# A Hymba-style encoder layer in split fp32r: one later norm sum, one more f with merged products, and two down units moved to the end of an f

## The chip, the cores and the metric

One core of one Trainium2 chip. The time is device time in microseconds for one execution, the median of 3 runs. Beside the runs there is one profiled execution, from which every view is taken; its times are given from the start of its span.

## The reference, cut to what matters

The kernel computes one encoder layer on 512 tokens of width 2048 and a last RMSNorm, all in float32. The first half (a norm, one input projection, a convolution group and a neighbourhood attention group, an output projection) is left as it is. What the change touches is the gated MLP behind it:

```
xn = rms_norm(x, ffn_norm_g)                 # 512 x 2048
up = xn @ w_up                               # 512 x 11264, gate half and value half
up = depthwise_conv(up, ffn_dw_w, ffn_dw_b)  # width 3 along the tokens
gate, val = split(up)
x = x + (silu(gate) * val) @ w_down          # 5632 -> 2048
return rms_norm(x, final_norm_g)
```

## The kernel before, in words

**Split operands.** Each float32 factor is split into a high part (rounded to fp32r) and a low part (the rest), and a product is three matmuls: high by high, high by low, low by high. For a weight unit (128 x 1024 numbers, 512 KB) ScalarE makes the high part `whi` (L117) and VectorE the low part `wlo` (L121). There are four buffers of each. `weights()` (L158) hands out units in the order of the list `plan` and makes each three units ahead of its use.

**The up projection.** The 5632 columns of each half are 44 tiles of 128, called f (0 to 43); eleven chunks c of four f (i = 0 to 3) share a down projection. For one f, the gate and the value tile by the two halves of the depth and of the tokens are combined into seven products, 0 to 6, as in Strassen's scheme as Winograd writes it; seven combinations `comb[c]` of the input stand in SBUF, each with high and low part beside each other, 256 columns each. A product has eight steps k over the depth. Three of the seven weight units are sums of loaded ones, made under names `ws` and `raw`: unit 1 and 2 by L712 and L714, unit 4 by L719, unit 6 by L723, on VectorE. Where f is 4 or less, `sums()` (L694 to L698) lets DMAs that add do the first two.

**Two forms of a product.** `up_apart` (L853) uses three matmuls of 256 columns for each k (lines 131, 135 and 136): high by high, high by low, low by high, all into one half of a PSUM bank. `up` (L764) is the merged form: one matmul of 512 columns by the high part (L774, "wides") gives high by high in the left half of the bank and high by low in the right half, and one of 256 columns (L780, "lows") adds low by high to the right half. Each product then comes out as two halves that are still to be added; that takes more copies on ScalarE (L810) and more additions on VectorE (L825 to L849, against L884 to L890). In the merged form the products are in runs that open together: (0,1), (2,3), (4,5), (6) for f under 4, and (0,1,2,3), (4,5,6) from f=4 on. The high matmuls of all products of a run come first (of the last one only the first), then the low ones product by product, each followed by the rest. f=0 and f=3 use `up_apart`, all others `up`.

**Gating.** `gated_tile` (L906) multiplies by the second norm's factor `rstd2` (L907, L908), does the width-3 convolution (L897 on ScalarE, L898 and L899 on VectorE), the SiLU (L910) and the product (L911). `in_two` (L914) splits the result into `hh` (L916, ScalarE) and `hl` (L917, VectorE). In the first chunk all four are split behind f=3.

**The down projection.** A down unit is one weight unit and two of the 16 output tiles d: 16 matmuls with the high weights (L934, hh and hl in turn), 8 with the low ones (L944), then for each d a copy out of PSUM (L946, ScalarE) and a DMA from POOL's queue that adds it to `x2d` in DRAM (L947). The two PSUM banks come from the tag `tr` (L924). `down_units(c, i, at)` (L732) says which units of the chunk before come behind product `at` of the f with index i; the same function places their weights in `plan`. Up to the last chunk one unit stands behind product 3 and one behind product 6 of each f.

**The second norm.** `stats2` (L678) runs beside f=0: behind each product `tick` (L141) lets it go one step. At the third step it adds two loaded sums (L684) and splits the result (L189, L190); after `rest` further steps two matmuls by ones (L194) sum over the partitions, and ScalarE and VectorE make `rstd2` (L198 to L205).

**What sets the order.** Each engine works off its own queue in order. A planner orders the queues beforehand, by the order of the code as priority and by costs and due times that it assumes; only instructions that are pinned, and those that `issue_after` ties to a matmul, are fixed by hand. The PE instructions of the up and down projections are not pinned. Loads of weights are on SP's queue (L112).

Of the kernel before, what the change touches and what calls it, by code (L numbers as in the profile page):

```python
# [17 lines left out]
D = 2048  # L18
# [24 lines left out]
CH = 4  # L43
# [23 lines left out]
def layer(ctx: ExitStack, tc: tile.TileContext, xT, xG, xw, w_a, w_in, w_v, w_out, w_up, w_down, par, tab, g3, out, last_out):  # L67
# [17 lines left out]
    def t2(name, dt=F32):  # L85
        return tp.tile([P, S], dt, tag="t2k", name=name)
# [54 lines left out]
    def tick(behind, mid=False):  # L141

        for todo in (steps, asteps):
            while todo and mid == (todo is asteps and amid[0]):
                try:
                    with tc.issue_after(behind.ins):
                        at = next(todo[0])
                    if todo is asteps:
                        amid[0] = at == "mid"
                    break  # L150
                except StopIteration:
                    todo.pop(0)
# [5 lines left out]
    def weights():  # L158
        at = weights.at
        weights.at += 1  # L160
        while len(made) < min(at + 1 + AHEAD, len(plan)):
            made.append(plan[len(made)]())
        return made[at]
# [21 lines left out]
    def spread(acc, to, n, name, bank, hold=False, both=False):  # L185

        m = to.stop - to.start
        h, l = (t2("n" + c, F32R)[:, :m] for c in "hl")
        nc.scalar.activation(h, acc[:, to], AF.Copy)  # L189
        nc.vector.tensor_sub(l, acc[:, to], h.bitcast(F32))  # L190
        yield
        ps = bank()[:, :m]
        for i, x in enumerate((h, l)):
            x = nc.tensor.matmul(ps, ones_r, x, start=i == 0, stop=i == 1)  # L194
            if i or hold:
                pin(x)
        r, q = t2(name)[:, :m], t2("q")[:, :m]
        nc.scalar.activation(r, ps, AF.Abs_reciprocal_sqrt, scale=1.0 / n, bias=eps)  # L198
        nc.vector.scalar_tensor_tensor(q, r, -0.5 / n, r, op0=ALU.mult, op1=ALU.mult)
        nc.vector.scalar_tensor_tensor(q, ps, n * EPS, q, op0=ALU.add, op1=ALU.mult)  # L200
        if both:
            nc.vector.scalar_tensor_tensor(ps, q, 1.5, r, op0=ALU.add, op1=ALU.mult)
            nc.scalar.activation(r, ps, AF.Copy)
            return ps, r
        nc.vector.scalar_tensor_tensor(r, q, 1.5, r, op0=ALU.add, op1=ALU.mult)  # L205
        return r

    def stat_bank(free=False):
        if free:
            return psa.tile([P, 2, S], F32, tag="sc", name="st")[:, 0]  # L210
        return psa.tile([P, S], F32, tag="po", name="st")

    def factor(acc, n, name, rest=1, free=False):
        steps = spread(acc, slice(0, S), n, name, lambda: stat_bank(free))
        next(steps)
        for _ in range(rest):
            yield
        try:
            next(steps)
        except StopIteration as e:  # L220
            return e.value
# [24 lines left out]
    for k in range(KD):  # L246
        if k < CH:
            raw = t4([P, U * P], "raw")
            n = S + 2 * P + (0 if k else KD)
# [3 lines left out]
        else:  # L253
            if k % CH == 0:
                raw = t4([P, U * P], "raw")
            if k % CH == 0 or k == CH + 2:
                o, n = 2 * (k % CH) * P, 2 * (2 if k < 2 * CH else CH) * P
# [22 lines left out]
    for step in ORDER:  # L280
# [5 lines left out]
        i = next(a_ if step == "a" else q_)  # L286
# [280 lines left out]
    p, n = -1, 0  # L567
# [104 lines left out]
    rstd2 = []  # L672
# [5 lines left out]
    def stats2():  # L678
        acc2, q = t2("acc2"), t2("sq")
        nc.sync.dma_start(acc2, sq2[0])  # L680
        nc.sync.dma_start(q, sq2[1])
        yield
        yield
        nc.vector.tensor_add(acc2, acc2, q)  # L684
        rstd2.append((yield from factor(acc2, D, "rstd2", rest=2, free=True)))

    def factors(f):

# [43 lines left out]
    def down_units(c, i, at):  # L732

        n = U // CH
        if not c:
            return ()
        if c < NCH - 1:
            return {3: (4 * i,), 6: (4 * i + n,)}.get(at, ())
        return {(1, 3): (0,), (1, 6): (2,), (2, 3): (4,), (2, 6): (6,), (3, 6): range(8, KD, n)}.get((i, at), ())
# [10 lines left out]

    out_half(mb, after)
    steps.append(stats2())

    def product_bank(f, c):

        n = 7 * f + c
        at = n % 6 if f < CH else 3 * (c % 3 == 0 and c > 0)
        if at < 3:
            return psm.tile([P, S], F32, tag="mm", name="pu")
        if at == 3:  # L760
            return psa.tile([P, S], F32, tag="po", name="pu")
        return psa.tile([P, S], F32, tag="tr", name="pu", bufs=2)

    def up(f, between):  # L764

        opened = {}
        runs = ((0, 1), (2, 3), (4, 5), (6,)) if f < CH else ((0, 1, 2, 3), (4, 5, 6))

        def bank(c):
            return product_bank(f, c)  # L770

        def wides(c, w, ps, ks, stop=False):
            for k in ks:
                i = nc.tensor.matmul(ps, w[0][:, k * P:(k + 1) * P], comb[c][k], start=k == 0,  # L774
                                     stop=stop and k == ks[-1])
            return i

        def lows(c, w, ps, stop=False):
            for k in range(U):
                i = nc.tensor.matmul(ps[:, H:], w[1][:, k * P:(k + 1) * P], comb[c][k][:, :H], start=False,  # L780
                                     stop=stop and k == U - 1)
            return i

        def product(c):

            w = weights()
            run = next(r for r in runs if c in r)
            if len(run) == 1:
                ps = bank(c)
                wides(c, w, ps, range(U - 1))  # L790
                lows(c, w, ps)
                i = wides(c, w, ps, range(U - 1, U), stop=True)
            elif c == run[-1]:
                ps = opened.pop(c)
                lows(c, w, ps)
                i = wides(c, w, ps, range(1, U), stop=True)
            else:
                if c == run[0]:
                    for j in run:
                        opened[j] = bank(j)  # L800
                        wides(j, w if j == c else made[weights.at + j - c - 1], opened[j],
                              range(1 if j == run[-1] else U))
                ps = opened.pop(c)
                i = lows(c, w, ps, stop=True)
            tick(i)
            between(c)
            return ps[:, :H], ps[:, H:]

        def copy(to, ps):
            nc.scalar.activation(to, ps, AF.Copy)  # L810

        def pair(name):
            return t2(name).rearrange("p (i t) -> p i t", i=2)

        def both(x):
            return x.unsqueeze(1).broadcast_to([P, 2, H])


        vv, low = pair("vv"), pair("pl")
        for i in range(2):  # L820
            m, l = product(i)
            copy(vv[:, i], m)
            copy(low[:, i], l)
        m7, l = product(2)
        add(vv, vv, low)  # L825
        low = pair("pl")
        copy(low[:, 0], l)
        m1, l = product(3)
        copy(low[:, 1], l)
        uu, v = pair("uu"), pair("vl")  # L830
        u, u2 = uu[:, 0], uu[:, 1]
        add(u2, m7, low[:, 0])
        add(v, vv, both(u2))
        m6, l = product(4)
        add(u, m1, low[:, 1])
        low = pair("pl")
        copy(low[:, 0], l)
        add(u2, u, m6)
        m2, l = product(5)
        add(u2, u2, low[:, 0])  # L840
        add(v, v, both(u2))
        add(vv[:, 1], vv[:, 1], u2)
        low, g = pair("pl"), pair("g")
        copy(low[:, 0], l)
        add(g[:, 0], u, m2)
        m3, l = product(6)
        copy(low[:, 1], l)
        add(g[:, 1], vv[:, 1], m3)
        add(g, g, low)  # L849
        g, v = (t.rearrange("p i t -> p (i t)") for t in (g, v))  # L850
        return g, v
# [49 lines left out]
        return y  # L901

    def hidden(f, between):
        return gated_tile(f, *(up_apart if f == CH - 1 else up)(f, between))

    def gated_tile(f, g, v):  # L906
        nc.vector.tensor_mul(g, g, rstd2[0])  # L907
        nc.vector.tensor_mul(v, v, rstd2[0])  # L908
        g, v = conv3(g, f), conv3(v, NF + f)
        nc.scalar.activation(g, g, AF.Silu)  # L910
        nc.vector.tensor_mul(g, g, v)  # L911
        return g
# [38 lines left out]
    def behind(c, i, at):  # L951
        if c == NCH - 1 and (i, at) == (0, 3):
            pend[-1] = in_two(pend[-1])
        down(pend, down_units(c, i, at))
# [23 lines left out]
    n = CH  # L978
# [47 lines left out]
    for d in range(KD):  # L1026
# [3 lines left out]
        i = nc.vector.tensor_add(x2[d][:, fm], x2[d][:, fm], ps)  # L1030
# [24 lines left out]
    for g, ps in enumerate(banks):  # L1055
# [5 lines left out]
        for k in range(n):  # L1061
# [3 lines left out]
            i = nc.tensor.matmul(ps, hh[:, tm], dh, start=False, stop=False)  # L1065
# [104 lines left out]
```

## Time and profile before

| | us |
|---|---|
| median of 3 runs | 2012.88 |
| lowest, highest | 2012.29, 2012.9 |
| the profiled execution's own time | 2013.73 |
| its span, first to last instruction | 2011.8 |
| f=0 begins, f=4 begins (first matmul) | 661.84, 742.97 |

In rows of the timeline the first number is the start, the second how long the group lasts, then engine, line, operation, what it writes and reads, shapes, and how many are grouped; in brackets stands the idle time of the engine ahead of it and what ended that. PE is TensorE's matmuls, PEld its weight loads, DVE is VectorE, ACT ScalarE, POOL GpSimd, SP SyncE. Matmuls overlap, so the printed length of one is longer than the distance to the next. In rows of windows come the stretch, its length, the busy time and instruction count of PE, PEld, DVE, ACT and POOL, the clock granted to TensorE, the share of the DMA engines and GB/s.

### The profile page before, as it was taken

What the parts mean: (1) busy time and instruction counts of PE and PEld (TensorE: products, weight loads), DVE (VectorE), ACT (ScalarE), POOL (GpSimd) and SP (SyncE); (2) the same over time, 40 slices, a digit from 0 to 9 for tenths busy, and PEclk for the clock granted to TensorE, in tenths of its full rate; (3) what the DMA queues carried; (4) which work ended last, traced back from release to release, by engine and by line L of the source; (5) the groups of instructions that cost most, each with busy time, mean ns of one, the idle gap of its engine ahead of it and who ended that gap; (6) DMA issues with size and microseconds to landing.
All of it is one profiled execution on the core that took longest, in us unless ns stands there. A gap on an engine that the chain in (4) does not pass through costs nothing.

```text
span 2011.8 us, 28094 instructions
## 1 busy us (share of the span) xinstructions
PE 2001.2 (99%) x10510; PEld 1716.8 (85%) x10510; DVE 1659.2 (82%) x2264; ACT 1065.7 (53%) x1689; POOL 171.1 (9%) x201
## 2 busy tenths in 40 slices
PE   9999999999999999999999999999999999999998
PEld 8888888888888898888888888888888888888887
DVE  7996888988576898887888888888887888888875
ACT  6323344476356665555655555564655655555563
POOL 0000000000002101111111111111111111110111
PEclk9999999999999999999999999999999999999999
DMA  7232323346348765555556555555555565564574
GB/s 258 84 105 92 112 96 110 105 138 209 104 136 211 187 159 156 135 136 149 132 133 149 134 134 148 135 136 147 133 139 147 131 142 147 131 142 126 147 200 136
DMA packets 98567, 284.25 MB, mean 141 GB/s; under 512 B 11008, under 2 KB 11520, under 8 KB 98432
## 3 DMA queue, kind: packets, MB, share of 16 engines
q1 hardware_dynamic: 71712, 231.07, 36.0%
q0 software_dynamic: 26720, 51.40, 16.8%
q8 instruction: 83, 1.36, 0.3%
q14 instruction: 52, 0.43, 0.1%
HBM read 227.90 MB, written 54.53 MB: 140 GB/s over the span
## 4 chain that ended last, share of the span: by engine, by line
PE 97%; DMA 1%; DVE 0%; ACT 0%; issue 0%; ACTq 0%; POOL 0%; POOLq 0%; DVEq 0%; SPq 0%
PE pu L774 27%; PE pu L780 14%; PE pd L934 14%; PE pd L944 7%; PE pj L131 6%; PE pj L135 6%; PE pj L136 6%; PE po L131 3%; PE po L135 3%; PE po L136 3%; PE pv L341 1%; PE pv L340 1%; PE pv L342 1%; PE pd L136 1%; PE pd L135 1%; PE pd L131 1%
## 5 line engine op out<-in xcount | busy, mean ns | idle before, releaser
L117 ACT ACTIVATE whi<-raw 128x1024 fp32r<-128x1024 f32 x364 | 384.8, 1058 | 537.6 <-PE pd L934 138.5
L121 DVE TENSOR_TENSOR wlo<-raw,whi 128x1024 fp32r<-128x1024 f32 x364 | 444.6, 1222 | 224.6 <-PE pu L780 101.2
L774 PE MATMUL pu<-xc,whi 128*128 128x512 f32 x2352 | 562.8, 390 | 0.0
L774 PEld LDWEIGHTS pu<-xc,whi 128*128 128x128 f32 x2352 | 435.9, 188 | 87.0 <-issue 0.2
L780 PEld LDWEIGHTS pu<-xc,wlo 128*128 128x128 f32 x2352 | 293.9, 192 | 6.8
L780 PE MATMUL pu<-xc,wlo 128*128 128x256 f32 x2352 | 296.1, 283 | 0.0
L934 PE MATMUL pd<-hl,whi 128*128 128x512 f32 x608 | 236.5, 389 | 0.0
L934 PE MATMUL pd<-hh,whi 128*128 128x512 f32 x608 | 236.5, 389 | 0.0
L947 POOL DMA_DIRECT2D x2d<-pdc x160 | 140.6, 895 | 1093.1 <-ACT pdc L946 1086.1
L131 PE MATMUL pj<-xh,whi 128*128 128x512 f32 x512 | 198.4, 392 | 0.1
L136 PE MATMUL pj<-xh,wlo 128*128 128x512 f32 x512 | 198.2, 390 | 0.0
L135 PE MATMUL pj<-xl,whi 128*128 128x512 f32 x512 | 198.2, 390 | 0.0
L117 ACT ACTIVATE whi<-ws 128x1024 fp32r<-128x1024 f32 x132 | 140.0, 1061 | 102.6 <-PE pu L774 54.2
L810 ACT ACTIVATE pl<-pu 128x256 f32<-128x256 f32 x294 | 111.4, 380 | 125.3 <-PE pu L774 88.0
L396 DVE SCALAR_TENSOR_TENSOR y<-ch,prm,y 128x501 f32<-128x501 f32 (+14 forms) x240 | 173.8, 743 | 4.4
L121 DVE TENSOR_TENSOR wlo<-ws,whi 128x1024 fp32r<-128x1024 f32 x132 | 161.3, 1222 | 3.3 <-ACT whi L117 1.9
L944 PE MATMUL pd<-hh,wlo 128*128 128x512 f32 x608 | 150.1, 389 | 0.0
L934 PEld LDWEIGHTS pd<-hl,whi 128*128 128x128 f32 x608 | 114.1, 188 | 23.8 <-DVE hl L917 0.2
L944 PEld LDWEIGHTS pd<-hh,wlo 128*128 128x128 f32 x608 | 114.1, 188 | 23.7
L934 PEld LDWEIGHTS pd<-hh,whi 128*128 128x128 f32 x608 | 114.1, 188 | 23.6
L131 PEld LDWEIGHTS pj<-xh,whi 128*128 128x128 f32 x512 | 96.0, 188 | 20.9 <-ACT whi L236 0.3
L136 PEld LDWEIGHTS pj<-xh,wlo 128*128 128x128 f32 x512 | 96.1, 188 | 20.5
(234 smaller groups left out, 2774.7 us busy)
## 6 DMA issues: line engine op xcount, KB each, us to landing
raw<-in_w_up SPq DMA_DIRECT2D x176, 512.0 KB, 3.6
raw<-in_w_down SPq DMA_DIRECT2D x88, 512.0 KB, 4.0
x2d<-pdc POOLq DMA_DIRECT2D x160, 256.0 KB, 4.9
raw<-in_w_in SPq DMA_DIRECT2D x60, 512.0 KB, 3.6
raw<-in_w_out SPq DMA_DIRECT2D x32, 512.0 KB, 3.6
raw<-in_w_v SPq DMA_DIRECT2D x16, 512.0 KB, 4.1
tab<-in_tab SPq DMA_DIRECT2D x32, 256.0 KB, 4.9
x<-in_xT SPq DMA_DIRECT2D x16, 256.0 KB, 5.6
```

What stands on the lines that cost most here:

```text
L117: i = nc.scalar.activation(hi[:, :n], raw[:, :n], AF.Copy)
L121: j = nc.vector.tensor_sub(lo[:, :n], raw[:, :n], hi[:, :n].bitcast(F32))
L131: m = nc.tensor.matmul(ps, hi[:, a], mh, start=start, stop=False)
L135: nc.tensor.matmul(ps, hi[:, a], ml, start=False, stop=False)
L136: return nc.tensor.matmul(ps, lo[:, a], mh, start=False, stop=stop)
L396: nc.vector.scalar_tensor_tensor(y[:, a:b], h[:, a + j - PAD:b + j - PAD], prm[:, o + j:o + j + 1], y[:, a:b], op0=ALU.mult, op1=ALU.add)
L774: i = nc.tensor.matmul(ps, w[0][:, k * P:(k + 1) * P], comb[c][k], start=k == 0, stop=stop and k == ks[-1])
L780: i = nc.tensor.matmul(ps[:, H:], w[1][:, k * P:(k + 1) * P], comb[c][k][:, :H], start=False, stop=stop and k == U - 1)
L810: nc.scalar.activation(to, ps, AF.Copy)
L934: nc.tensor.matmul(ps, w[0][:, a], x, start=k + i == 0, stop=False)
L944: nc.tensor.matmul(ps, w[1][:, a], hs[k][0], start=False, stop=k == CH - 1)
L947: nc.gpsimd.dma_start(xd[d], t, accum_op=ALU.add)
```

## The change

Three edits. The factor of the second norm waits three steps and not two between the split and the two matmuls that sum it, so these matmuls come one product later in f=0. f=3 uses the merged form `up` like the others, and only f=0 stays in `up_apart`. And in the second chunk's first f (f=4) both down units, 0 and 2, stand behind product 6, where the first of them stood behind product 3; their weights move in `plan` likewise. Behind the edit in `down_units` the lines of the new kernel are two further down.

```
-        rstd2.append((yield from factor(acc2, D, "rstd2", rest=2, free=True)))
+        rstd2.append((yield from factor(acc2, D, "rstd2", rest=3, free=True)))
...
     def down_units(c, i, at):
         n = U // CH
         if not c:
             return ()
+        if c == 1 and not i:
+            return (0, n) if at == 6 else ()
         if c < NCH - 1:
             return {3: (4 * i,), 6: (4 * i + n,)}.get(at, ())
...
     def hidden(f, between):
-        return gated_tile(f, *(up_apart if f == CH - 1 else up)(f, between))
+        return gated_tile(f, *up(f, between))
```

More of the change, by code (lines that the diff above doesn't have):

```diff
@@ L684, in stats2 @@
         nc.vector.tensor_add(acc2, acc2, q)
-        rstd2.append((yield from factor(acc2, D, "rstd2", rest=2, free=True)))
+        rstd2.append((yield from factor(acc2, D, "rstd2", rest=3, free=True)))
     def factors(f):
@@ L736, in down_units @@
             return ()
+        if c == 1 and not i:
+            return (0, n) if at == 6 else ()
         if c < NCH - 1:
@@ L903, in hidden @@
     def hidden(f, between):
-        return gated_tile(f, *(up_apart if f == CH - 1 else up)(f, between))
+        return gated_tile(f, *up(f, between))
     def gated_tile(f, g, v):
```

## The prediction

> **What bounds the kernel now.** I read the page's busy times first, then the chain that ended last.
>
> ```profile
> PE 2001.2 (99%) x10510; PEld 1716.8 (85%) x10510; DVE 1659.2 (82%) x2264; ACT 1065.7 (53%) x1689; POOL 171.1 (9%) x201
> PE 97%; DMA 1%; DVE 0%; ACT 0%; issue 0%; ACTq 0%; POOL 0%; POOLq 0%; DVEq 0%; SPq 0%
> ```
>
> TensorE is busy 99% of 2011.8 us and is 97% of the chain, so a change can win only by giving it less to do or by closing one of its few waits. An 82% VectorE looks idle enough, but that is a mean over stages. The table of windows, cut where the first f's begin, shows the stretch that the diff touches (columns: stretch, length, busy time of PE, PEld, DVE, ACT, POOL):
>
> ```profile
> 703.40:722.90 19.50, 19.50 (x114) 17.22 (x113) 18.89 (x27) 11.47 (x19) 1.73 (x2) 1.00 0.65 170
> 722.90:743.00 20.10, 20.10 (x170) 20.10 (x169) 19.53 (x27) 10.21 (x14) 1.74 (x2) 1.00 0.73 190
> 743.00:773.40 30.40, 30.40 (x163) 26.15 (x162) 30.03 (x40) 18.65 (x29) 1.78 (x2) 1.00 0.52 150
> 773.40:803.70 30.30, 30.30 (x161) 26.22 (x160) 24.64 (x32) 16.73 (x25) 3.50 (x4) 1.00 0.56 140
> ```
>
> These are f=2, f=3, f=4 (with two down units) and f=5. VectorE is full up to 773.4 (30.03 of 30.40 us) and has 5.66 us to spare from f=5 on. So here two engines are bound together, and what matters is by how much VectorE's weight parts come ahead of TensorE's use of them.
>
> **The norm's sum.** The timeline of PE, and of DVE, at the end of the fifth product of f=0:
>
> ```profile
> 676.11 0.28 PE L136 MATMUL pu<-xc,wlo 128*128 128x256 f32 x1
> 676.65 0.49 PE L194 MATMUL st<-nh,ones 128*128 128x512 f32 x1 [0.26 <-ACT nh L189]
> 677.72 0.50 PE L194 MATMUL st<-nl,ones 128*128 128x512 f32 x1 [0.58 <-DVE nl L190]
> 678.06 0.28 PE L131 MATMUL pu<-xc,whi 128*128 128x256 f32 x1
> ...
> 675.24 0.69 DVE L684 TENSOR_TENSOR acc<-acc,sq 128x512 f32<-128x512 f32 x1 [1.96 <-DMA sq<-sq]
> 678.25 1.22 DVE L121 TENSOR_TENSOR wlo<-ws,whi 128x1024 fp32r<-128x1024 f32 x1
> ```
>
> TensorE's price per matmul is the distance of starts, not the printed length:
>
> ```profile
> 687.80 3.82 PE L774 MATMUL pu<-xc,whi 128*128 128x512 f32 x16
> 691.45 2.08 PE L780 MATMUL pu<-xc,wlo 128*128 128x256 f32 x16
> ...
> 722.81 0.28 PE L131 MATMUL pu<-xc,whi 128*128 128x256 f32 x1
> 742.97 5.86 PE L774 MATMUL pu<-xc,whi 128*128 128x512 f32 x25
> ```
>
> Sixteen 512-wide ones take 691.45-687.80 = 3.65 us, 0.228 each. All of f=3, apart, is 7x24 matmuls of 256 columns in 742.97-722.81 = 20.16 us, 0.120 each. From 676.11 to 678.06 are 1.95 us; undisturbed it would be 0.12+2x0.228 = 0.58. The two sum matmuls thus hold TensorE up 1.37 us, because their input comes from a sum that landed by DMA at 675.2. One product later is 676.23+24x0.12 = 679.11, after nl was there (it released the matmul at 677.72): the wait goes whole, **-1.37 us**. What is late next: the seventh product's low part ends at 678.25+1.22 = 679.47, and TensorE would use it at 679.11+0.46+0.24 = 679.81, 0.34 us later. It just fits. rstd2 then comes some 1.4 us later at most; its first readers (L907, L908 for f=0) are far enough behind, and VectorE has other work in between.
>
> **The fourth f merged.** Per k two 256-wide matmuls become one of 512: 2x0.120-0.228 = 0.012 us, 56 times, 0.67 us. I take **-0.67 us**. The page "TensorE: Matmul & The Clock Gate" of the Trainium skill (section "Wait — 56ns, not 53.3ns?") states a time of N/2.4 ns plus about 2.5 ns for each matmul, by which the merge would save only 2.5 ns each, 0.14 us in all (an estimate from that page). The rows give 0.120 us for 256 columns where the page's rule gives 0.109, so the measurement decides.
>
> In exchange there are more additions. Issue distances of VectorE, from the timeline in f=2:
>
> ```profile
> 707.15 0.69 DVE L849 TENSOR_TENSOR g<-g,pl 128x512 f32<-128x512 f32 x1
> 707.75 1.22 DVE L719 TENSOR_TENSOR ws<-ws,raw 128x1024 f32<-128x1024 f32 x1
> ...
> 719.85 1.23 DVE L121 TENSOR_TENSOR wlo<-raw,whi 128x1024 fp32r<-128x1024 f32 x1
> 720.98 0.42 DVE L838 TENSOR_TENSOR uu<-uu,pu 128x256 f32<-128x256 f32 x1
> 721.31 1.23 DVE L121 TENSOR_TENSOR wlo<-ws,whi 128x1024 fp32r<-128x1024 f32 x1
> ```
>
> So 0.60 us for 512 columns, 0.33 for 256, 1.13 for a weight unit. Merged, an f has 4 wide and 7 narrow additions (4.71 us); apart, 2 and 4 (2.52 us): VectorE gets **2.19 us more**, in the stretch where it is full. ScalarE gets six more copies of 0.38 us, 2.3 us, beside 10.21 us of work in 20.10: hidden.
>
> ```profile
> L810 ACT ACTIVATE pl<-pu 128x256 f32<-128x256 f32 x294 | 111.4, 380 | 125.3 <-PE pu L774 88.0 <-PE pu L780 33.1 <-DMA x2d<-pdc 1.1
> ```
>
> **Both down units at the end of f=4.** The work stays the same; the order changes. First the rows of f=4 (PE; then DVE and ACT):
>
> ```profile
> 754.11 0.39 PE L934 MATMUL pd<-hh,whi 128*128 128x512 f32 x1
> ...
> 759.60 4.02 PE L774 MATMUL pu<-xc,whi 128*128 128x512 f32 x17
> 763.45 3.04 PE L780 MATMUL pu<-xc,wlo 128*128 128x256 f32 x24
> ...
> 771.57 1.98 PE L944 MATMUL pd<-hh,wlo 128*128 128x512 f32 x8
> 773.38 1.98 PE L774 MATMUL pu<-xc,whi 128*128 128x512 f32 x8
> ...
> 710.18 1.23 DVE L121 TENSOR_TENSOR wlo<-ws,whi 128x1024 fp32r<-128x1024 f32 x1 [0.61 <-ACT whi L117]
> 737.48 0.42 DVE L886 TENSOR_TENSOR uu<-uu,pu 128x256 f32<-128x256 f32 x1 [0.54 <-PE pu L136]
> 752.01 1.22 DVE L121 TENSOR_TENSOR wlo<-raw,whi 128x1024 fp32r<-128x1024 f32 x1
> 754.89 0.68 DVE L917 TENSOR_TENSOR hl<-uy,hh 128x512 fp32r<-128x512 f32 x1
> 757.23 1.22 DVE L723 TENSOR_TENSOR ws<-ws,raw 128x1024 f32<-128x1024 f32 x1
> 758.48 1.06 ACT L117 ACTIVATE whi<-ws 128x1024 fp32r<-128x1024 f32 x1 [3.78 <-DVE ws L723]
> ...
> 772.78 0.58 ACT L946 ACTIVATE pdc<-pd 128x512 f32<-128x512 f32 x1
> ```
>
> The moved down unit is the 759.60-754.11 = 5.49 us of TensorE between product 3 and product 4. It also was the time in which VectorE caught up. The tightest unit is the seventh (made by L723, then whi, then wlo). Its high part is ready at 758.48+1.06 = 759.54, and TensorE first uses it with the last of the 17 matmuls, at 759.60+16x0.228 = 763.25: 3.7 us to spare.
>
> After the change TensorE wants it 5.49 us earlier for the missing down unit, and 2.04 us earlier for the two gains: 755.72. VectorE reaches L723 at 757.23+2.19-1.13 (the down unit's low part of 752.01, now behind) and, where its two idle moments of 0.61 and 0.54 close, 1.15 sooner: 757.14. The high part then is there at 759.45, **3.7 us late** if every queue keeps the order of the code. Two things can shorten that. The low matmuls of products 4 and 5, 16x0.12 = 1.92 us, need nothing from it and can be queued ahead; the planner, which orders each queue before the run, has done this once, in f=40:
>
> ```profile
> 1844.54 5.40 PE L774 MATMUL pu<-xc,whi 128*128 128x512 f32 x23
> 1849.78 0.63 PE L780 MATMUL pu<-xc,wlo 128*128 128x256 f32 x4
> 1850.38 0.47 PE L774 MATMUL pu<-xc,whi 128*128 128x512 f32 x1
> ```
>
> Here four low matmuls stand ahead of the last of 24 high ones (the rest of product 3 and the 17 that open products 4 to 6), where the code has all the low ones behind it. And the four hl of L917 (4x0.60 = 2.4 us, the last at 754.89) no longer have to be ready at 754: behind L723 they would bring it to 754.7 and leave 1.3 us of lateness. So the cost lies between 0 (both) and 3.7 (neither; 4.9 if the idle moments stay). I take one of them, **+1.9 us**.
>
> A second new wait: the two units now follow each other in the two banks of L924. The second's first matmul needs the first's eviction, which began 1.21 us after the eight low matmuls did (772.78 against 771.57) and ended at 773.36, when they were over at 773.38. So it is 0 with ScalarE free and up to 1.06 with a whi ahead of the copy; I take **+0.1**. The moved unit's SP load (512 KB) and its two POOL transfers of 0.9 us have idle queues around them: POOL is busy 1.78 of 30.40 us.
>
> **Sum:** -1.37-0.67+1.9+0.1 = -0.04 us on the span of 2011.8 (2013.73 for the profiled execution, 0.85 above the median). On the median of 2012.88 that is **2012.8**, no change.
>
> **Rivals.**
> - **The gain survives whole** (low matmuls ahead and hl behind): -2.04+0.1, so 2010.9. For it: no deadline asks for hl before 760 any more. Against it: hl is issued ahead of the later units in the code.
> - **VectorE becomes the bound, slower**: the order of the code, a 3.7 us wait ahead of the high matmul of f=4's seventh unit and 0.3 at the bank: -2.04+4.0 = +2.0, 2014.9 (to 2016.1 with the idle moments unclosed). It decides when L723 starts after 753.4 (755.72 less the 1.25 to whi's start and its 1.06) and nothing is put ahead. For it: DVE's 30.03 of 30.40. Against it: the row of 1849.78.
> - **The wait slows TensorE's clock**: at the start sixteen 256-wide matmuls took 3.50 us, 0.219 each against 0.120, while the granted clock reads 1.00. If a wait of 3.7 us brought that rate back for so many, it adds 16x0.099 = 1.6: 2016.5. The same page of the Trainium skill (section "What's actually happening") says that an idle window of about 3.4 us halves the clock until the engine has again been busy as long. No wait of that length stands in this trace's FFN, so nothing here tests it.
>
> ```profile
> 1.10:4.60 3.50, 3.50 (x16) 3.29 (x16) 0.49 (x2) 1.64 (x4) 0.38 (x2) 1.00 0.81 268
> ```
>
> - **The moved sum gives nothing**: the 0.34 us of room at the seventh product of f=0 goes to a queue shuffle, and -1.37 becomes some -0.3: 2013.9.
>
> **How the numbers follow.** Forecast 0.42, whole gain 0.20, VectorE bound 0.22, slow clock 0.07, sum without gain 0.09. The range is 2010.5 to 2016.0: below lies little of the whole gain (2010.9), above it most of the slow clock and the far end of the second rival, some 0.15 together. A measurement of this kernel tells about 0.2% (4.0 us) from no change. A gain over 4.0 us isn't there to be had, since the waits and matmuls named hold 2.0: 0.02. A loss over 4.0 us takes half of the slow clock's chance (its 3.6 us and a little more) and the far end of the second rival (a wait over 6 us at the seventh unit, with the bank's 1.06 on top): 0.04 and 0.06, so 0.10. The rest, 0.88, is within.
>
> **What would show it.** The profile after should have the st matmuls at 679.1 without a wait, f=3 in 19.45 us, VectorE full until f=5. Then look at f=4's seventh product: a PE wait named for whi L117 is the second rival, low matmuls ahead of it the forecast, no wait the first. A wait on ACT pdc ahead of the second down unit prices the bank. I am wrong if waits appear in f=2 or f=3, where the sixth and seventh units have little room, or if hl, not a weight part, holds the down units.

## The result, and the profile after

The changed kernel takes 2020.55 us (median of 6 runs, 2019.48 to 2021.8), the kernel before 2012.87 beside it (6 runs, 2012.29 to 2013.4): a ratio of 1.0038, 95% interval 1.0028 to 1.0048. That is 7.7 us slower, outside the range of 2010.5 to 2016.0. The profiled execution of after took 2020.29 us with a span of 2018.4; lines of the new kernel from `down_units` on are two further down (L774 is now L776, L810 L812, L835 L837).

The page of after, first the busy times and then TensorE's costliest group (its last columns: busy time, mean ns, idle time ahead of it and what ended most of that):

```profile
PE 2002.2 (99%) x10454; PEld 1714.7 (85%) x10454; DVE 1660.5 (82%) x2269; ACT 1066.2 (53%) x1695; POOL 171.2 (8%) x201
...
L776 PE MATMUL pu<-xc,whi 128*128 128x512 f32 x2408 | 578.1, 391 | 5.6 <-ACT pl L812 2.9
```

TensorE has 56 matmuls fewer, VectorE 5 instructions and ScalarE 6 more, as foretold. New are 5.6 us of idle time ahead of the high matmuls, half of them ended by a copy of ScalarE. The timeline of TensorE, from the norm's sum on, shows where they stand:

```profile
679.16 0.39 PE L194 MATMUL st<-nh,ones 128*128 128x512 f32 x1
679.39 0.39 PE L194 MATMUL st<-nl,ones 128*128 128x512 f32 x1
...
740.75 6.08 PE L776 MATMUL pu<-xc,whi 128*128 128x512 f32 x26
746.67 4.00 PE L782 MATMUL pu<-xc,wlo 128*128 128x256 f32 x32
750.50 1.78 PE L776 MATMUL pu<-xc,whi 128*128 128x512 f32 x7
755.16 5.54 PE L776 MATMUL pu<-xc,whi 128*128 128x512 f32 x16 [2.88 <-ACT pl L812]
763.39 0.47 PE L776 MATMUL pu<-xc,whi 128*128 128x512 f32 x1 [2.70 <-DVE uu L837]
763.70 3.03 PE L782 MATMUL pu<-xc,wlo 128*128 128x256 f32 x24
766.57 1.78 PE L776 MATMUL pu<-xc,whi 128*128 128x512 f32 x7
768.18 0.39 PE L936 MATMUL pd<-hh,whi 128*128 128x512 f32 x1
...
773.66 0.50 PE L936 MATMUL pd<-hh,whi 128*128 128x512 f32 x1
...
779.23 5.83 PE L776 MATMUL pu<-xc,whi 128*128 128x512 f32 x25
```

The first 26 high matmuls are the last of f=3 and 25 of f=4, so f=4 begins 0.23 us into that row, at 740.98, against 742.97 before: 1.99 us were gained. It ends at 779.23 against 773.38: 5.85 us late, so f=4 lost 7.84. From there on the two timelines run 5.85 us apart to the last matmul. The rest of the 6.56 us between the two profiled executions came behind it (9.2 us to the end of the span, against 8.5); the medians differ by more, since the profiled execution of before lay 0.86 above its median.

In f=4 the loss is four terms. The seven matmuls from 750.50 on should be followed at 750.50+7x0.228 = 752.10, and the sixteen of products 4 and 5 start at 755.16: **3.06 us**, released by ScalarE's copy L812. These sixteen take 5.54 us where sixteen took 3.82 in f=1: **1.72**. The first matmul of product 6 follows 2.86 us late, released by VectorE's L837: **2.86**. The rest (0.08 behind that, 0.14 at the second down unit) is **0.22**. Together 7.86, against the 7.84 read from the starts of f=4 and f=5.

Neither release is a weight part. They free banks of PSUM. From f=4 on, products 0, 1, 2, 4, 5 share three banks and products 3 and 6 share one (L759, the tag `po`), so product 4 needs the bank of product 0, emptied by ScalarE's copies L812, and product 6 that of product 3, emptied when VectorE's L837 has read it. ScalarE in after, then in before:

```profile
751.65 0.62 ACT L912 ACTIVATE uy<-uy 128x512 f32<-128x512 f32 x1
752.17 1.14 ACT L918 ACTIVATE hh<-uy 128x512 fp32r<-128x512 f32 x2
753.93 0.63 ACT L918 ACTIVATE hh<-uy 128x512 fp32r<-128x512 f32 x1 [0.62 <-DVE uy L913]
754.46 0.37 ACT L812 ACTIVATE vv<-pu 128x256 f32<-128x256 f32 x1
754.73 0.38 ACT L812 ACTIVATE pl<-pu 128x256 f32<-128x256 f32 x1
```

```profile
752.07 0.37 ACT L810 ACTIVATE vv<-pu 128x256 f32<-128x256 f32 x1
752.33 0.38 ACT L810 ACTIVATE pl<-pu 128x256 f32<-128x256 f32 x1
```

In before the bank of product 0 came free at 752.7 and nobody asked for it till 759.60, behind the down unit. In after TensorE asks at 752.10, and the copies stand behind the rounding L918 of f=3's gated tile, which waits for VectorE's product L913. VectorE's timeline in after, then its one row of before that matters:

```profile
756.14 1.23 DVE L723 TENSOR_TENSOR ws<-ws,raw 128x1024 f32<-128x1024 f32 x1
757.28 0.70 DVE L919 TENSOR_TENSOR hl<-uy,hh 128x512 fp32r<-128x512 f32 x1
757.88 1.23 DVE L712 TENSOR_TENSOR ws<-raw 128x1024 f32<-128x1024 f32 x1
759.01 0.70 DVE L827 TENSOR_TENSOR vv<-vv,pl 128x512 f32<-128x512 f32 x1
759.62 0.43 DVE L834 TENSOR_TENSOR uu<-pu,pl 128x256 f32<-128x256 f32 x1
759.95 1.23 DVE L121 TENSOR_TENSOR wlo<-ws,whi 128x1024 fp32r<-128x1024 f32 x1
761.08 0.69 DVE L835 TENSOR_TENSOR vl<-vv,uu 128x512 f32<-128x512 f32 x1
761.68 1.23 DVE L121 TENSOR_TENSOR wlo<-raw,whi 128x1024 fp32r<-128x1024 f32 x1
762.82 0.43 DVE L837 TENSOR_TENSOR uu<-pu,pl 128x256 f32<-128x256 f32 x1
```

```profile
761.05 0.42 DVE L835 TENSOR_TENSOR uu<-pu,pl 128x256 f32<-128x256 f32 x1
```

VectorE never rests here: each instruction begins as the one before it gives way. L837 is done at 763.25 because eight others stand ahead of it, whatever TensorE does. In before the same addition ended at 761.47, and TensorE wanted the bank at 763.25. In after it wanted it at 760.5, though it had lost nearly 5 us by then.

### The profile page after: what moved, and what is told of

It is laid out like the page before. It is cut to its first block, busy times and chain, and to the rows that moved or that the text cites. A ratio compares the mean times of both kernels' runs of the same rounds, so it can differ in the third digit from the quotient of the medians.

```text
span 2018.4 us, 27994 instructions
## 1 busy us (share of the span) xinstructions
PE 2002.2 (99%) x10454; PEld 1714.7 (85%) x10454; DVE 1660.5 (82%) x2269; ACT 1066.2 (53%) x1695; POOL 171.2 (8%) x201
## 4 chain that ended last, share of the span: by engine, by line
PE 62%; ACT 0%; DVE 0%; ACTq 0%; issue 0%; DVEq 0%
PE pu L776 25%; PE pd L936 14%; PE pu L782 13%; PE pd L946 7%; PE pd L135 1%; PE pd L136 1%; PE pd L131 1%; PE pt L1071 0%; PE pt L1067 0%; PE pt L1070 0%; PE pt L1059 0%; ACT xg L1091 0%; ACT sq L1074 0%; ACTq L1167 0%; PE st L194 0%; DVE uu L837 0%
## 5 line engine op out<-in xcount | busy, mean ns | idle before, releaser
L776 PE MATMUL pu<-xc,whi 128*128 128x512 f32 x2408 | 578.1, 391 | 5.6 <-ACT pl L812 2.9
L776 PEld LDWEIGHTS pu<-xc,whi 128*128 128x128 f32 x2408 | 447.2, 189 | 95.8 <-ACT pl L812 3.3
L782 PEld LDWEIGHTS pu<-xc,wlo 128*128 128x128 f32 x2408 | 301.2, 191 | 7.1
L782 PE MATMUL pu<-xc,wlo 128*128 128x256 f32 x2408 | 303.4, 283 | 0.0
L812 ACT ACTIVATE pl<-pu 128x256 f32<-128x256 f32 x301 | 113.7, 379 | 124.4 <-PE pu L776 84.9
```

## The experiments

**The theories.** A: the moved down unit was the cover for two PSUM banks that ScalarE and VectorE free late, and they are late enough to hurt only when the merged f=3 has loaded VectorE too; so two edits meet. B: one edit alone makes the loss (at first the merged f=3, later the norm's sum). C: the releaser named is only the last of several, and a weight part or VectorE itself holds TensorE. D: VectorE has simply too much work there, in whatever order.

**One edit alone, and pairs of them.** Each is the kernel before with the lines named.

`norm_only`, only the norm's sum one product later:

```
-        rstd2.append((yield from factor(acc2, D, "rstd2", rest=2, free=True)))
+        rstd2.append((yield from factor(acc2, D, "rstd2", rest=3, free=True)))
```

> Only the norm's sum comes one product later; f=3 apart and the down units as before. Both theories: the two sum matmuls stand without a wait (-1.37 us), but VectorE is full up to f=4, so part of it comes back where a low part or hl is late (the seventh unit of f=3 had 0.56 us to spare, hl of f=3 came 0.2 us ahead of use). 2011.5 if nothing comes back, 2012.5 if nearly all does; I expect 2012.1.

`merge_only`, only f=3 merged:

```
-        return gated_tile(f, *(up_apart if f == CH - 1 else up)(f, between))
+        return gated_tile(f, *up(f, between))
```

> Only f=3 merged (VectorE +2.19 us); the norm and the down units as before. Theory A (the moved down unit uncovered the wait for PSUM banks that ScalarE and VectorE free late): the loss here is only hl of f=3 coming some 2 to 3 us late for the first down unit, +1.5 to +2.3, 2014.4 to 2015.2. Theory B (the merged f=3 alone makes the loss, wherever the down units stand): +5 us or more, 2018 and up.

`down_only`, only the down units moved:

```
+        if c == 1 and not i:
+            return (0, n) if at == 6 else ()
```

> Only the two down units at the end of f=4; the norm and f=3 apart as before. Theory A: product 6 of f=4 waits for the bank that L837 frees; with 2.19 us less on VectorE than in the changed kernel L837 ends near 760.4, TensorE wants the bank at 757.8, so +2.5 us, 2015.4, with the wait named uu L837. Theory B: within 0.3 us of before, 2012.9.

`norm_merge`, `merge_down` and `norm_down` are the pairs of these.

> The norm's sum later and f=3 merged, the down units as before. Theory A: VectorE bounds the stretch up to hl of f=3, so the 1.37 us of the norm are worth nothing here: as merge_only within 0.6 us, 2014.0 to 2015.2. Theory B: 2017 or more.

> Merged high parts in f=3 and the moved down units, the norm's sum at its old place. Theory A (two small edits meet: f=3's shorter product time leaves VectorE a queue of work, and without the down unit between its products f=4 waits for PSUM banks that ScalarE and VectorE free late): VectorE's queue fixes when the bank of product 3 comes free, so the norm's sum is worth nothing and the time is that of all three edits, 2020.5, give or take 0.7, with waits of about 3 us ahead of products 4 and 6 of f=4. Theory B (a cause in the third edit, the norm's): the time falls to about 2014, the sum of merged parts alone (2014.2) and down units alone (2013.9) over before (2012.7) being some 2015.4.

> The norm's sum one product later and the moved down units, f=3 with its products apart as before: the pair of edits that is still missing. Theory A (the loss needs the merged f=3 and the moved down units together): as down units alone, 2013.9, between 2012.8 and 2015, with waits of 1 us or less ahead of product 4 of f=4. Theory B (the norm's sum takes part in the loss): 2017 or more.

The medians, the ratios to before with their 95% intervals, and from TensorE's timeline the time from the first matmul of f=4 to the first of f=5, with the waits ahead of products 4 and 6 (the 0.2 of two kernels is for the high weights of product 6, all others are for banks). Each ratio is to before as measured beside that kernel, where its median lay between 2012.70 and 2013.02:

| kernel | us | ratio | f=4 | product 4 | product 6 |
|---|---|---|---|---|---|
| before | 2012.87 | 1 | 30.41 | 0 | 0 |
| norm_only | 2012.77 | 0.9999 (0.9990 to 1.0008) | 30.44 | 0 | 0 |
| merge_only | 2014.24 | 1.0006 (0.9998 to 1.0015) | 31.94 | 0 | 0 |
| down_only | 2013.85 | 1.0007 (0.9998 to 1.0016) | 31.59 | 0.69 | 0.2 |
| norm_merge | 2013.88 | 1.0006 (0.9997 to 1.0015) | 31.35 | 0 | 0 |
| norm_down | 2013.99 | 1.0007 (0.9998 to 1.0016) | 31.58 | 0.68 | 0.2 |
| merge_down | 2021.05 | 1.0041 (1.0028 to 1.0054) | 39.12 | 1.32 | 4.48 |
| after | 2020.55 | 1.0038 (1.0028 to 1.0048) | 38.25 | 3.06 | 2.86 |

No edit alone, and no pair with the norm's sum, is distinguishable from before, though `merge_only`, `down_only` and the two pairs read 1.1 to 1.5 us above it and their f=4 is longer by 0.9 to 1.5. `norm_only`, for which I had expected 2012.1, gains nothing. The merged f=3 and the moved down units together make the whole loss: B falls in both forms. Two details were missed. In `merge_only` and `norm_merge` the down unit behind product 3 waits 0.7 to 1.2 us in all for hl of L917, which is the wait on hl that the prediction named as a sign against itself. And in `down_only` I had expected a wait on L837; TensorE and VectorE there show why it didn't come:

```profile
753.51 3.94 PE L776 MATMUL pu<-xc,whi 128*128 128x512 f32 x16 [0.52 <-ACT pl L812]
757.30 0.99 PE L782 MATMUL pu<-xc,wlo 128*128 128x256 f32 x7
758.31 0.50 PE L776 MATMUL pu<-xc,whi 128*128 128x512 f32 x1
```

```profile
752.47 0.68 DVE L919 TENSOR_TENSOR hl<-uy,hh 128x512 fp32r<-128x512 f32 x1
...
757.08 0.42 DVE L834 TENSOR_TENSOR uu<-pu,pl 128x256 f32<-128x256 f32 x1
757.42 0.41 DVE L837 TENSOR_TENSOR uu<-pu,pl 128x256 f32<-128x256 f32 x1
```

With f=3 apart, VectorE has done the last hl at 753.15 (in after at 757.98) and L837 at 757.83 (763.25). Besides, seven low matmuls stand ahead of the high one of product 6, the very move that the forecast had counted on; in after there is none, since all 24 low ones stand behind it.

`merge_down` loses as much as after, though by other parts:

```profile
753.80 3.92 PE L776 MATMUL pu<-xc,whi 128*128 128x512 f32 x16 [1.16 <-ACT pl L812]
762.04 0.77 PE L776 MATMUL pu<-xc,whi 128*128 128x512 f32 x1 [4.32 <-DVE uu L837]
762.61 5.32 PE L782 MATMUL pu<-xc,wlo 128*128 128x256 f32 x24
767.73 1.85 PE L776 MATMUL pu<-xc,whi 128*128 128x512 f32 x7
```

Product 4 waits only 1.3 us and its matmuls keep their pace, so TensorE asks for the bank of product 6 earlier and waits 4.48. I had expected about 3 us at each. (In its profile the norm's loaded sum came in time, in after it came late; `late_add` takes that up.) Then 24 low matmuls take 5.32 us and not 3.03, at half the clock (the clock is the third number from the end):

```profile
762.00:765.00 3.00, 2.96 (x13) 2.89 (x14) 1.42 (x2) 0.38 (x1) 0.00 (x0) 0.50 0.80 264
```

**Another bank for product 6.** The changed kernel with one line more or less; the order on every engine stays. In `psm6` product 6 takes the bank of product 2, in `sc6` one that nothing else uses (the tag `sc`). The expectation speaks of a six-bank pool; the pool has three banks.

```
-        at = n % 6 if f < CH else 3 * (c % 3 == 0 and c > 0)
+        at = n % 6 if f < CH else 3 * (c % 3 == 0 and c > 0 and (f, c) != (CH, 6))       # psm6
+        at = n % 6 if f < CH else 6 if (f, c) == (CH, 6) else 3 * (c % 3 == 0 and c > 0)  # sc6
...
+            return psa.tile([P, 2, S], F32, tag="sc", name="pu")[:, 0] if at == 6 else ...  # sc6
```

> The changed kernel, but product 6 of f=4 takes the bank of the six-bank pool that product 2 had, which VectorE frees with the addition of product 2 (760.05 us in the profile of after), and no longer the bank of product 3 (freed at 763.25); the order of instructions on every engine is unchanged. Theory A: product 6 starts at about 760.1 instead of 763.39, and the low part of its weights (761.18) is there before the low matmuls come: some 3.2 us less, 2017.3. Theory C (the wait is for VectorE's weight parts or for anything else that comes late at that place, and the bank is only the last named): less than 0.7 us, 2020 to 2020.5.

> The changed kernel, but product 6 of f=4 takes a bank that nothing else uses at that time, so that it waits for no bank at all; the order of instructions on every engine is unchanged. Theory A: product 6 starts when its high part is there or product 5 is done, about 758.9 in place of 763.39, and then its low matmuls wait till 761.2 for the low part at most: some 4.2 us less than after, 2016.2. What is left over before (3.5 us) is the first wait, ahead of product 4 (3.0 us), and the slower matmuls behind it (1.7 us). Theory C: less than 0.7 us.

`psm6` took 2015.70 (ratio to before 1.0017, 1.0008 to 1.0025), `sc6` 2015.75 (1.0013, 1.0005 to 1.0022): both are about 4.8 us faster than after and still slower than before, so the bank was the holder of the second wait and C falls. TensorE in `psm6`, then in `sc6`:

```profile
753.29 3.92 PE L776 MATMUL pu<-xc,whi 128*128 128x512 f32 x16 [1.17 <-ACT pl L812]
758.32 0.47 PE L776 MATMUL pu<-xc,whi 128*128 128x512 f32 x1 [1.11 <-DVE uu L834]
```

```profile
755.56 5.67 PE L776 MATMUL pu<-xc,whi 128*128 128x512 f32 x17 [2.96 <-ACT pl L812]
761.08 3.04 PE L782 MATMUL pu<-xc,wlo 128*128 128x256 f32 x24
```

The second wait is now named by L834, as expected, and in `sc6` it is gone. The first wait is 1.3 us in the one profile and 3.1 in the other, though the queues are the same; why is told with `late_add`. In the profile of `sc6`, whose first wait is about that of after, f=4 takes 35.30 us against 38.25: 2.95 less, the second wait of 2.86. That `psm6` gained 1.6 us more than I had expected fits the short first wait of its profile, since I had counted with that of after. Six of its eleven runs lie between 2015.1 and 2015.7, and the profiled one is among them. Four lie between 2017.2 and 2018.0, about where I had expected it (2017.3).

**The split later.** `latehl`: the changed kernel, with the gated tiles of f=0 to f=3 rounded and split behind product 5 of f=4 rather than ahead of its copies.

```
-        if c == NCH - 1 and (i, at) == (0, 3):
-            pend[-1] = in_two(pend[-1])
+        if (c, i, at) in ((NCH - 1, 0, 3), (1, 0, 5)):
+            pend[:] = [h if isinstance(h, tuple) else in_two(h) for h in pend]
...
-            hs = [h if isinstance(h, tuple) else in_two(h) for h in hs]
+            hs = [h if isinstance(h, tuple) or not c else in_two(h) for h in hs]
```

> The changed kernel, but the four gated tiles of f=0 to f=3 are rounded and split behind product 5 of f=4 and no longer behind product 3, so that ScalarE makes its copies of products 0 to 2 ahead of those roundings, and VectorE the additions of products 2 and 3 ahead of the four subtractions. Theory A: no wait for a bank ahead of product 4 and no slow clock behind it, the bank of product 3 is free by about 757; the split tiles now come 2 to 3 us late for the first down unit. Time about 2014, between 2012.8 and 2015. Theory D (VectorE has simply too much work in f=2 to f=4, in whatever order): the wait only moves to the split tiles, and the time stays at 2018 or above.

2012.91 us (2011.95 to 2013.99), ratio to before 1.0000 (0.9991 to 1.0009): the whole loss is gone with no work removed, so D falls. TensorE no longer stops in f=4:

```profile
750.28 5.40 PE L776 MATMUL pu<-xc,whi 128*128 128x512 f32 x23
755.52 1.11 PE L782 MATMUL pu<-xc,wlo 128*128 128x256 f32 x8
756.47 0.40 PE L776 MATMUL pu<-xc,whi 128*128 128x512 f32 x1
756.71 2.08 PE L782 MATMUL pu<-xc,wlo 128*128 128x256 f32 x16
```

The seven high matmuls that stood alone at 750.50 in after now run on into the sixteen of products 4 and 5. The addition that frees the bank of product 3 is done at 754.92, where after has 763.25:

```profile
754.51 0.41 DVE L837 TENSOR_TENSOR uu<-pu,pl 128x256 f32<-128x256 f32 x1
```

The late split tiles, for which I had allowed 2 to 3 us, cost nothing either: the planner put three high matmuls of f=5 among those of the down unit.

**Pairs in f=4.** `pairs4`: the changed kernel, with f=4 run in pairs, as the f before it, on seven free banks.

```
-        at = n % 6 if f < CH else 3 * (c % 3 == 0 and c > 0)
+        at = n % 6 if f < CH else (4, 5, 0, 0, 0, 3, 6)[c] if f == CH else 3 * (c % 3 == 0 and c > 0)
...
-        runs = ((0, 1), (2, 3), (4, 5), (6,)) if f < CH else ((0, 1, 2, 3), (4, 5, 6))
+        runs = ((0, 1), (2, 3), (4, 5), (6,)) if f <= CH else ((0, 1, 2, 3), (4, 5, 6))
```

> The changed kernel, but f=4 makes its products in pairs, as the f before it do, and takes seven banks that are free at that time, so that no product of f=4 waits for a bank, while VectorE's and ScalarE's work stays what it is. Theory A: the two waits and the slow clock go; what is left is at most 1 to 2 us for the parts of the last weight unit. Time 2012.6, between 2011.5 and 2014.5. Theory D (VectorE has simply too much work in f=2 to f=4): the waits move to the parts of the weights or to the split tiles, 2016 or more.

2014.08 (2012.35 to 2015.26), ratio 1.0004 (0.9995 to 1.0013), 1.5 us above the expected middle and inside its range. No wait for a bank is left; what shows now are the weight parts that the prediction had looked for. Counted by starts the two waits are 0.5 and 1.3 us, together about the 1.9 of its sum:

```profile
756.18 1.22 PE L782 MATMUL pu<-xc,wlo 128*128 128x256 f32 x8 [0.37 <-DVE wlo L121]
...
761.73 1.21 PE L782 MATMUL pu<-xc,wlo 128*128 128x256 f32 x8 [0.83 <-DVE wlo L121]
```

**The norm's addition later.** `late_add` is `latehl` with the addition of the two loaded sums one step later, and the matmuls where the change has them:

```
         yield
         yield
+        yield
         nc.vector.tensor_add(acc2, acc2, q)
-        rstd2.append((yield from factor(acc2, D, "rstd2", rest=3, free=True)))
+        rstd2.append((yield from factor(acc2, D, "rstd2", rest=2, free=True)))
```

> The kernel with the late split, and besides the addition that ends the norm's sum one step later in VectorE's queue, its matmuls where the change has them. In four of ten profiles VectorE stood 1.4 to 2.6 us at this addition, for a DMA that landed late, and had no idle time to make it up by f=4. Theory E (this DMA makes the spread of the times): VectorE now stands 0.6 us at most, the slower half of the executions goes, and the median falls from 2012.9 to about 2012.2. Rival (the spread is of the last transfers, or of something else): 2012.9 as before.

2012.50 us, ratio 0.9998 (0.9989 to 1.0007). All 11 runs lie between 2012.06 and 2012.76, where `latehl` had 2011.95 to 2013.99 and before, beside this one, 2012.06 to 2014.25 in 27 runs. The spread fell to a third, as theory E wants, on eleven runs; that the median fell is within the interval and not shown. The addition in VectorE's timeline, in after, in `sc6` and in `late_add`:

```profile
675.06 0.69 DVE L684 TENSOR_TENSOR acc<-acc,sq 128x512 f32<-128x512 f32 x1 [1.72 <-DMA sq<-sq]
```

```profile
675.48 0.69 DVE L684 TENSOR_TENSOR acc<-acc,sq 128x512 f32<-128x512 f32 x1 [2.55 <-DMA sq<-sq]
```

```profile
675.41 0.69 DVE L685 TENSOR_TENSOR acc<-acc,sq 128x512 f32<-128x512 f32 x1
```

In `psm6`, `merge_down` and `latehl` the sum was there in time and VectorE didn't wait. Where it did wait, VectorE was that much later for the next 80 us: the product L913 that releases the last L918 begins at 753.20 in after and at 751.35 in `psm6`. That is the difference between a first wait of 3 us and one of 1.3. With f=3 apart the delay was made up: `norm_down` stood 1.04 us at the addition and `down_only` not at all, and L913 begins at 748.38 and 748.40.

This is the best version found: it beats after by some 8 us (2012.50 against 2020.55, each measured beside before), and it can't be told from before.

## Why the prediction was wrong, step by step

- **The norm's sum, -1.37.** The mechanism was right: the matmuls start at 679.16 (679.1 foretold) without a wait. The size was that of one execution. The profiled execution of before was itself one in which the loaded sum came late, and its time lay 0.85 above the median, which I had noted and not used. In the profiles of `down_only` and `merge_down` the sum matmuls stand at their old place, the sum came in time, and they run at 676.31 and 676.64 without a wait: there the edit has nothing to gain. `norm_only` gives no gain that can be seen, by its interval between 2.0 us faster and 1.6 slower.
- **The fourth f merged, -0.67.** f=3 takes 19.50 us in after (19.45 foretold), with VectorE full, as the windows show (the first row is f=3, the second the sixteen matmuls behind the first wait; columns as in the prediction):

```profile
721.50:741.00 19.50, 19.50 (x114) 17.22 (x113) 19.50 (x28) 11.34 (x20) 1.74 (x2) 1.00 0.72 185
...
755.20:760.60 5.40, 5.40 (x16) 4.05 (x16) 5.40 (x8) 3.92 (x7) 0.00 (x0) 0.68 0.28 94
```

  So these two steps held in this execution: f=4 began 1.99 us earlier, 2.04 foretold. Of VectorE's 2.19 us more the page shows 1.3 over the whole span (1659.2 to 1660.5 busy); what took the rest was not looked into.
- **Both down units at the end, +1.9: this step failed.** It said of the moved unit: "It also was the time in which VectorE caught up", and then asked only which weight part would be late: "The tightest unit is the seventh". That unit's high part was ready at 758.46, a microsecond earlier than I had worked out, and TensorE came to use it at 763.39:

```profile
757.40 1.06 ACT L117 ACTIVATE whi<-ws 128x1024 fp32r<-128x1024 f32 x1 [1.48 <-DVE ws L723]
```

  The lateness that I had priced was there, but hidden: without the waits for banks TensorE would have asked for that part at 752.10+16x0.228 = 755.75, 2.7 us too early. What I left out is that the down unit covered two banks as well. The same queue of VectorE held the additions that empty PSUM, and ScalarE's held copies that do so; I traced neither. The bounds of "between 0 (both) and 3.7" were bounds for one resource. Measured were 3.06 and 2.86 for two banks and 1.72 for the slow matmuls, 7.6 where I took 1.9. Of the two reliefs that I weighed, low matmuls put ahead did not come in after, and of the four hl only the last came behind L723; the first came in `down_only`, the second had to be written by hand in `latehl`, and it was enough.
- **The second down unit's bank, +0.1.** Right: 0.14. I looked for a bank where two down units follow each other and not where two products do.
- **The rivals.** "VectorE becomes the bound" had the right engine and the wrong thing waited for, and its price of 2.0 above before was about a quarter of the loss. "The wait slows TensorE's clock" came true on top of it, with its 1.6 us (1.72 measured), but I had given it 0.07 as a case of its own rather than as a consequence of a long wait wherever it comes from. The chance of a loss over 4.0 us, 0.10, was far too small: the range left out that two waits can stand one behind the other.
- **The sum of the parts.** I added up terms of edits that meet in one queue. The two that lose together cost 1.5 and 1.1 us alone, which their intervals don't tell from nothing; `merge_down` costs 8.

## What to carry to other kernels

Before moving a block of matmuls away from between two others, list everything that the block covers: weight parts, and also every PSUM bank that the next product takes over, with the engine that empties it and what stands ahead of that in its queue. Where an engine is full, price edits together and not one by one, and look for a reorder in that queue (here the split behind the additions) before taking work away. A stall read from one profiled execution, above all behind a DMA, is worth its size there only; a run with that edit alone, or several profiles, tell its usual size.

## What the runs showed of the hardware

- After waits of about 3 us the matmuls were slow for a while. In after the granted clock is 0.50 in the first 3.40 us behind the 3.06 us wait and 0.99 in the next 1.90; in `sc6`, behind 3.13 us, it is 0.51 and then 1.00, and in `merge_down`, behind 4.48, 24 low matmuls took 5.32 us. Behind the 2.86 us wait of after they took their usual 3.03, and behind 1.3 us in `psm6` sixteen took 3.92. The Trainium skill ("TensorE: Matmul & The Clock Gate", section "What's actually happening") puts the idle window at about 3.4 us; here waits of 3.06 and 3.13 us were enough, and the measurement decides.
- The wait's place seems to count beside its length. By the clock records of these traces the half clock lasted 3.41 us in after (from 755.22) and in `sc6`, and 6.83 in `merge_down`, and the full clock before it lasted 750.93, 750.93 and 754.35 us, which is 220, 220 and 221 times 3.413. So each change of the clock here lay on a grid of 3.41 us. The wait of 3.06 us in after (752.10 to 755.16) lies inside one step of that grid, from 751.80 to 755.22. The wait of 2.86 us (760.53 to 763.39) is cut by the grid at 762.04, 1.5 us of it in one step and 1.35 in the next. That this is why it did no harm fits the figures, but no run tests it.
- Another bank for product 6 of f=4 was worth 4.8 us. The Trainium skill ("Perfetto Trace Analysis", section "Matmul Optimizations") advises to use all eight PSUM banks; `sc6`, which takes one that stood unused, agrees with it for this place. `psm6`, which takes one of the three that products 0 to 2 use and that comes free earlier, gained as much, and `latehl` shows that earlier emptying does as well.
- The same loaded sum let VectorE wait between 0 and 2.55 us from one execution to the next, and behind an engine without idle time that difference lasts for 80 us.
